# A two-layer diffusion backbone on one core: layer 1's weight sums over all of layer 0's MLP, two activation sums on VectorE, first down weights loaded early

## The chip, the core and the metric

The kernel runs on one core of a Trainium2 chip. The metric is the device time of the whole program in microseconds (us), as the median of several runs. The engines are named as in the profile: PE is TensorE's matrix multiplication and PEld its weight load, DVE is VectorE, ACT is ScalarE, POOL is GpSimd, and SP is SyncE, which in this kernel only issues transfers (DMAs). Each engine works through its own instructions in a fixed order and stops at one whose inputs or buffer are not ready; what stands behind it then waits too. "SPq" in a row of the profile is SP's queue of transfers.

## The reference, cut to what matters

A stream of 1024 latent tokens and one of 256 context tokens, 1024 channels wide, pass through two layers. Each layer has a mixer (left out here) and an MLP with a squared ReLU, 4096 hidden channels wide. Each sublayer is normalised, then scaled and shifted by a modulation that is itself a matrix product of the conditioning vectors with `w_mod`.

```python
def squared_relu_mlp(h, w1, w2):
    return jnp.square(jax.nn.relu(h @ w1)) @ w2
...
    for l in range(DEPTH):                       # DEPTH = 2
        mod_l = jnp.split((s_lat @ w_mod[l] + b_mod[l])[:, None, :], 6, axis=-1)
        mod_c = jnp.split(s_ctx @ w_mod[l] + b_mod[l], 6, axis=-1)
...
        x = x + mod_l[2] * y_l
        x = x + mod_l[5] * squared_relu_mlp(modulate(rmsnorm(x, g_norm[l, 1]), mod_l[3], mod_l[4]), w_ff1[l], w_ff2[l])
        if not last:                             # layer 0 alone: the context stream too
            xc = xc + mod_c[2] * y_c
            xc = xc + mod_c[5] * squared_relu_mlp(modulate(rmsnorm(xc, g_norm[l, 1]), mod_c[3], mod_c[4]), w_ff1[l], w_ff2[l])
    return rmsnorm(x, g_final)
```

## The kernel before, in words

**Layout and precision.** Activations lie channel by token: tiles of 128 channels and 512 tokens (token blocks `tb` 0 and 1, the latents) or 256 tokens (`tb` 2, the context). Every operand of a product is kept as two parts, a rounded one and the rest (`wsplit`: ACT makes the rounded copy at L110, DVE the difference at L111), and every product is three matmuls (`mm3`, L129 to L131).

**Layer 0's MLP** (`mlp`, L730 to L814). The 4096 hidden channels are 32 tiles, taken in 11 blocks: one of 2 tiles, then ten of 3. The first block is done token block by token block (the "lead"); the next nine are the loop `for blk in blocks[lead:-1]`; the last stands by itself. A block has two phases. In the up phase, for each hidden tile `hd`, `load` fetches its 0.5 MB of `w1` and of `w2`, each into a staging tile `st` and from there, split, into `wa` or `wb` (three buffers each), and `up` makes 128 hidden channels for the three token blocks: PE fills a bank `acc` (three of them), ACT does ReLU, square and the rounded copy (L749 to L752), DVE the difference (L753). In the down phase, for each of the 8 output tiles `fo`, `down` multiplies the block's three hidden tiles into a bank `ff` (four of them) for each token block, and DVE adds it to the residual stream (L710, `x<-ff,mod,x`). L710 has high priority, so in DVE's order it stands before side work that is written around it.

**Side work in the down phase.** Two generators are advanced by `next(...)` inside the loop over `fo`. `side` is `mods1()`: layer 1's modulation, six loads of 0.5 MB of `w_mod` per block (L97) and on DVE the products with the conditioning vectors (L181, L183). `sums` is `wsums()`: layer 1's MLP is computed with a seven-product scheme in the manner of Strassen, which needs sums of blocks of its weights. They are made here once, in 60 half-tiles: 16×2 of `w_ff1`, stored in DRAM as `su`, and 14×2 of `w_ff2`, stored as `sv`. One half-tile is two loads of 256 KB into a staging tile (L887 or L896), four additions on POOL in place (L903 to L906, 128x256 each), and a store of 512 KB (L890 or L898). SP issues all of them. In SP's queue the store waits until POOL is done, and whatever stands behind it in SP's order is issued only after it.

**One pool of staging tiles.** `st` has three buffers (`wp`, `bufs=3`), used in turn by every weight load, every `w_mod` load and every half-tile of the sums. A buffer comes free when its weight is split, when DVE has used its modulation weights, or when the half-tile's store has landed.

**Layer 1's MLP.** `right1` (L1229 to L1248) makes the seven right-hand operands out of the normalised activations `x[k, tb]`, k being a channel tile and `HK` half of the eight. `osplit` (L1207 to L1214) splits one into the rounded copy (ACT) and the difference (DVE, L1210, or L1213 where a shift is added). While this runs, PE already does the products of the first three "up units" (`lead`), operation by operation (`together`). A unit is one pair of hidden tiles through seven operations, named "1" to "7"; its left operands come through `left` (L1250 to L1280), a generator whose first step loads operations 1 and 2 and whose second loads 5/6 (as S1 and S2, into the single tile `ws`), 3 (S4) and 7/4 (S3 and A22). L1364 copies a finished product out of its bank, L1371 adds another to it, L1311 is the matmul. The up units end with unit 15, whose operations go in the order `LORDER`, and `down_unit` then does the down products by blocks `DBLK`. Layer 1's down operands come back from DRAM (`down_ops`, L1427 and L1430).

Of the kernel before, what the change touches and what calls it, by code (L numbers as in the profile page):

```python
# [9 lines left out]
F32 = mybir.dt.float32  # L10
# [7 lines left out]
P = 128  # L18
# [12 lines left out]
DBLK = ((0, 1), (2, 3, 4), (5, 6, 7), (8, 9, 10), (11, 12, 13))  # L31
NWP = 14
# [19 lines left out]
def trunk(tc, es, A, out):  # L52
    nc = tc.nc
    act, dve, pool, pe, sp = nc.scalar, nc.vector, nc.gpsimd, nc.tensor, nc.sync

    cst = es.enter_context(tc.tile_pool(name="cst", bufs=1))
    wp = es.enter_context(tc.tile_pool(name="wp", bufs=1))
# [282 lines left out]
    with ExitStack() as em, eg:  # L340
# [8 lines left out]
        for c, ks in [(c, (0, 1, 2, 3)) for c in range(3)] + [(c, (4, 5, 6, 7)) for c in range(3)] + \  # L349
                [(c, range(KT)) for c in range(3, NCH)]:  # L350
            tb, off = tok(c)
# [46 lines left out]
        for src, dst in ((LI, RI), (LF, RF)):  # L398
            for c0 in range(0, NCH, 4):
                n = min(4, NCH - c0)  # L400
# [280 lines left out]
        for g in range(3):  # L681
            v = v_proj0(g)
# [47 lines left out]
    def mlp(res, pf, pw, p2, tbs, h2, segs, finish, pre, lead, side, sums):  # L730


        l = res.l
        nh = A["ff1"].shape[1]
        first = nh % HB or HB
        blocks = [list(range(first))] + [list(range(b, b + HB)) for b in range(first, nh, HB)]

        def load(hd, w1, w2):
            if hd not in w1:
                w1[hd] = wload(A["ff1"][l, hd], (KT, P))  # L740
            if hd not in w2:
                w2[hd] = wload(A["ff2"][l, hd], (1024,), pw, "wb")

        def up(w1, tb):
            n = TBS[tb][1]
            ps = acc(n)
            proj(ps, w1, [h2[k, tb] for k in range(KT)])
            r = pf.tile([P, 512], F32, tag="s5", bufs=13, name="s5")[:, :n]
            act.activation(r, ps, AF.Relu)  # L749
            act.activation(r, r, AF.Square)  # L750
            hi, lo = actpair(tb, p2 if tb == 2 else pf, "s", (13, 3))
            act.copy(hi, r)  # L752
            dve.tensor_sub(lo, r, f(hi))  # L753
            passed(n / 100)
            return hi, lo

        def down(blk, w2, s, fo, seg, norm):
            tb, a, n = seg
            ps = aux("ff2")[:, :n]
            for j, hd in enumerate(blk):  # L760
                mm3(ps, tuple(t[:, fo * P:(fo + 1) * P] for t in w2[hd]), tuple(t[:, a:a + n] for t in s[hd, tb]),
                    j == 0, j == len(blk) - 1)
            res.update(ps, 5, fo, tb, norm, seg if norm else None)
            passed(len(blk) * n / 800)

        def ups(blk, w1, w2, s, tb):
            for hd in blk:
                load(hd, w1, w2)
                s[hd, tb] = up(w1[hd], tb)

        torder = list(dict.fromkeys(g[0] for g in segs))
        w1, w2, s = {}, {}, {}
        for i, tb in enumerate(torder):
            for bi, blk in enumerate(blocks[:lead]):
                if lead > 1:
                    w1, w2, s = {}, {}, {}
                if (0, tb) not in h2:
                    drain()
                ups(blk, w1, w2, s, tb)
                if bi == 0 and i + 1 < len(torder) and pre:  # L780
                    pre[torder[i + 1]]()
                for fo in range(KT):
                    down(blk, w2, s, fo, (tb, 0, TBS[tb][1]), False)
        for blk in blocks[lead:-1]:
            w1, w2, s = {}, {}, {}
            for hd in blk:
                load(hd, w1, w2)
                for tb in tbs:
                    s[hd, tb] = up(w1[hd], tb)
            for fo in range(KT):  # L790
                for _ in range(3):
                    next(side, None)
                for _ in range(2):
                    next(sums, None)
                for tb in tbs:
                    down(blk, w2, s, fo, (tb, 0, TBS[tb][1]), False)
        for _ in side:
            pass
        blk = blocks[-1]
        w1, w2, s = {}, {}, {}  # L800
        two = len(torder) == 2
        ups(blk, w1, w2, s, torder[0])
        for i, tb in enumerate(torder):
            if i + 1 < len(torder):
                ups(blk[:1] if two else blk, w1, w2, s, torder[i + 1])
            elif two:
                ups(blk[1:], w1, w2, s, tb)
            for seg in segs:
                if seg[0] == tb:
                    for fo in range(KT):  # L810
                        down(blk, w2, s, fo, seg, True)
                    norm_later(res.tot[seg], seg[2], acc if two and seg == segs[-1] else lone,
                               lambda r, seg=seg: finish(seg, r))
        drain()  # L814
# [12 lines left out]
    with ExitStack() as ef:  # L827
# [30 lines left out]
        for fo in range(5):  # L858
            w = ws[fo] if fo < 2 else wload(A["w_out0"][fo], (KT, P))
            for tb in (0, 1, 2):  # L860
                o, n = TBS[tb]
# [17 lines left out]
        def wsums():  # L879


            for j in range(16):
                for h in (0, 1):
                    t = wp.tile([P, 1024], F32, tag="st", bufs=3, name="st")
                    v = t.rearrange("p (i e n c) -> p i e n c", i=2, e=2, c=P)
                    for i in (0, 1):
                        sp.dma_start(v[:, i], A["ff1"][1, 2 * j + i].rearrange("p (e n) c -> p e n c", e=2)[  # L887
                            :, :, 2 * h:2 * h + 2])
                    wsum(v)
                    sp.dma_start(su[j, :, :, 2 * h:2 * h + 2], t.rearrange("p (s n c) -> p s n c", s=4, c=P))  # L890
                    yield
            for j in range(NWP):
                for h in (0, 1):
                    t = wp.tile([P, 1024], F32, tag="st", bufs=3, name="st")
                    for e in (0, 1):
                        sp.dma_start(t[:, e * 512:e * 512 + 512], A["ff2"][1, 2 * j + e, :, h * 512:h * 512 + 512])  # L896
                    wsum(t.rearrange("p (e n i c) -> p i e n c", e=2, i=2, c=P))
                    sp.dma_start(sv[j, h], t.rearrange("p (e n i c) -> p e n i c", e=2, i=2, c=P))  # L898
                    yield

        def wsum(v):
            a, b, c, d = v[:, 0, 0], v[:, 0, 1], v[:, 1, 0], v[:, 1, 1]
            pool.tensor_add(d, c, d)  # L903
            pool.tensor_sub(c, a, c)
            pool.tensor_sub(a, d, a)
            pool.tensor_sub(b, b, a)  # L906
# [322 lines left out]
    def right1(r):  # L1229

        x, d = res.x, {}
        for k in range(HK):
            scaled(k, 1, r)
            dve.tensor_sub(x[k, 0], x[k, 1], x[k, 0])
        B["5"] = [osplit(ap_, "a5", 32, x[k, 0]) for k in range(HK)]
        for k in range(HK):
            scaled(k + HK, 1, r)
            dve.tensor_sub(x[k, 0], x[k + HK, 1], x[k, 0])
        B["6"] = [osplit(po_, "o", NO, x[k, 0], shift(k + HK)) for k in range(HK)]
        B["3"] = [osplit(ap_, "a5", 32, x[k + HK, 1], shift(k + HK)) for k in range(HK)]  # L1240
        db = pf.tile([P, 16], F32, name="db")[:, 0:HK]
        dve.tensor_sub(db, mod[:, 1, 3, HK:KT, 0], mod[:, 1, 3, 0:HK, 0])
        for k in range(HK):
            pool.tensor_sub(x[k, 1], x[k + HK, 1], x[k, 1])
        B["7"] = [osplit(po_, "o", NO, x[k, 1], db[:, k:k + 1]) for k in range(HK)]
        for k in range(HK):
            pool.tensor_sub(x[k + HK, 0], x[k + HK, 0], x[k, 0])
        B["4"] = [osplit(ap_, "a2", 8, x[k + HK, 0]) for k in range(HK)]  # L1248

    def left(load, n, early=False):  # L1250
# [165 lines left out]
    def down_ops(blk, ops=WORDER):  # L1416

        nb = {}
        for op in ops:
            i = WORDER.index(op)  # L1420
            nb[op] = []
            for j in blk:
                at = (ap_, "a5", 32) if i < 4 else (po_, "o", NO)
                if i < NSPLIT:
                    w = tuple(at[0].tile([P, 512], F32R, tag=at[1], bufs=at[2], name=at[1]) for _ in range(2))
                    for e in range(2):
                        sp.dma_start(f(w[e]), f(sw[j, i, e]))  # L1427
                else:
                    v = px.tile([P, 512], F32, tag="t", bufs=5, name="t")
                    sp.dma_start(v, f(sw[j, i, 1]))  # L1430
                    w = osplit(*at, v)
                nb[op].append(w)
        return nb
# [53 lines left out]
    nxt = {}  # L1487
    for op in LORDER:
        u.run(op)
        if op == "2":  # L1490
            nxt.update(down_ops(DBLK[0], ("1", "5", "6", "3")))
        elif op == "6":
            d = down_unit(DBLK[0], 0, nxt)
            nxt.update(down_ops(DBLK[0], ("7", "2", "4")))
        elif op == "4":
            reload_x(0)
# [117 lines left out]
```

## Time and profile before

| | before |
|---|---|
| median of 3 runs | 3215.52 us (3210.82 to 3216.55) |
| the profiled execution | 3212.63 us |
| its span in the profile | 3210.9 us |
| PE busy | 2956.2 us, 92% |
| DVE busy | 1960.8 us, 61% |
| ACT busy | 1207.9 us, 38% |
| POOL busy | 310.4 us, 10% |
| bytes moved | 443.52 MB, mean 138 GB/s |
| mean granted PE clock | 0.963 |

How to read it: the span is what the profiler covers; 1.7 us of the profiled execution lie around it. A row of a view reads: time, engine, line of the code, operation, `out<-in` by the program's tile names, shape, and how often (xN); what stands in brackets is the idle time just before, and what ended it. A row of the waits reads: engine, tile and line that waited, what it waited for, then the total in us, the number of times and the longest.

### The profile page before, as it was taken

The numbers are of one execution on the slowest core, as the hardware profiler recorded it, in microseconds if no ns is written. First come the engines' busy times: TensorE is split into PE (matmuls) and PEld (weight loads), VectorE is DVE, ScalarE is ACT, GpSimd is POOL, SyncE is SP. The second block draws the span as 40 slices with busy tenths as digits, with TensorE's granted clock in tenths as the row PEclk, the third lists the DMA queues.
The fourth block names the chain that finished last, engine by engine and source line by source line (L and its number), as shares of the span: only waits on it lengthen the run. The fifth ranks groups of instructions, "written<-read, shape, count | busy, mean of one in ns | idle before, by whom it ended". The sixth has DMA issues, their size and how long they took to land.

```text
span 3210.9 us, 44648 instructions
## 1 busy us (share of the span) xinstructions
PE 2956.2 (92%) x16386; PEld 2479.8 (77%) x16386; DVE 1960.8 (61%) x3877; ACT 1207.9 (38%) x2660; POOL 310.4 (10%) x491
## 2 busy tenths in 40 slices
PE   6899999999966887999999979999999799998998
PEld 5787888788755776888888867787877578876887
DVE  5868687537343433444445568757577776656766
ACT  3335344424120221222224225556577454433332
POOL 0001011000444442000000000000000200000000
PEclk9999999999978988999999989999999899999999
DMA  6153334631565564222212143222532366687751
GB/s 207 44 161 110 109 119 148 201 103 33 164 203 184 179 203 169 79 79 66 71 58 82 56 148 95 90 74 82 178 102 96 107 223 237 240 296 225 252 183 70
DMA packets 303803, 443.52 MB, mean 138 GB/s; under 512 B 25712, under 2 KB 174816, under 8 KB 303584
## 3 DMA queue, kind: packets, MB, share of 16 engines
q1 hardware_dynamic: 300992, 436.74, 42.0%
q10 hardware_dynamic: 2592, 3.93, 0.3%
q8 instruction: 129, 2.11, 0.3%
q14 instruction: 90, 0.74, 0.1%
HBM read 330.08 MB, written 110.49 MB: 137 GB/s over the span
## 4 chain that ended last, share of the span: by engine, by line
PE 67%; DMA 12%; DVE 9%; POOL 6%; issue 3%; ACT 2%; SPq 1%; POOLq 0%; DVEq 0%; ACTq 0%
PE acc L131 9%; PE acc L129 9%; PE acc L130 9%; PE acc L1311 9%; PE bd L1311 7%; DMA st<-in_ff_dram 4%; PE ff L129 3%; PE po L1109 3%; PE ff L130 3%; PE ff L131 3%; PE S L1083 3%; DMA kd<-rh 2%; DMA qd<-rh 2%; PE pT L1104 2%; DMA su<-st 1%
## 5 line engine op out<-in xcount | busy, mean ns | idle before, releaser
L129 PE MATMUL acc<-a,wah 128*128 128x512 f32 (+1 forms) x1752 | 652.2, 372 | 36.8 <-ACT wah L110 21.9
L130 PE MATMUL acc<-a,wah 128*128 128x512 f32 (+1 forms) x1752 | 646.3, 369 | 0.0
L131 PE MATMUL acc<-a,wal 128*128 128x512 f32 (+1 forms) x1752 | 643.4, 368 | 0.0
L129 PEld LDWEIGHTS acc<-a,wah 128*128 128x128 f32 x1752 | 337.2, 192 | 87.1 <-ACT wah L110 25.9
L131 PEld LDWEIGHTS acc<-a,wal 128*128 128x128 f32 x1752 | 336.6, 192 | 47.5 <-DVE wal L111 0.5
L130 PEld LDWEIGHTS acc<-a,wah 128*128 128x128 f32 x1752 | 337.4, 193 | 45.6 <-issue 0.5
L129 PE MATMUL ff<-s,wbh 128*128 128x512 f32 (+1 forms) x768 | 280.8, 368 | 81.5 <-DVE x L710 81.5
L110 ACT CAST wah<-st 128x1024 fp32r<-128x1024 f32 (+4 forms) x129 | 120.5, 936 | 556.3 <-DMA st<-in_ff_dram 448.9
L130 PE MATMUL ff<-s,wbh 128*128 128x512 f32 (+1 forms) x768 | 277.7, 362 | 0.0
L131 PE MATMUL ff<-s,wbl 128*128 128x512 f32 (+1 forms) x768 | 276.5, 360 | 0.0
L710 DVE SCALAR_TENSOR_TENSOR x<-ff,mod,x 128x512 f32<-128x512 f32 (+1 forms) x264 | 172.0, 658 | 105.4 <-PE ff L131 103.7
L129 PEld LDWEIGHTS ff<-s,wbh 128*128 128x128 f32 x768 | 148.9, 194 | 108.6 <-DVE x L710 84.4
L111 DVE TENSOR_TENSOR wal<-st,wah 128x1024 fp32r<-128x1024 f32 (+4 forms) x129 | 138.7, 1077 | 137.7 <-ACT wah L110 137.4
L753 DVE TENSOR_TENSOR s<-s,s 128x512 fp32r<-128x512 f32 (+1 forms) x96 | 61.6, 644 | 242.5 <-ACT s L752 242.3
L1085 DVE TENSOR_REDUCE mx<-S 128x1 f32<-128x512 f32 (+1 forms) x288 | 165.4, 594 | 68.5 <-PE S L1083 67.1
L1091 ACT ACTIVATE p<-S,nm 128x512 f32<-128x512 f32 (+1 forms) x288 | 175.9, 620 | 45.1 <-DVE nm L1088 44.8
L1083 PE MATMUL S<-K,Q 128*128 128x512 f32 (+1 forms) x576 | 163.7, 384 | 14.7 <-ACT p L1091 8.2
L1311 PE MATMUL bd<-a,wbh 128*128 128x512 f32 x480 | 154.6, 403 | 18.0 <-ACT wbh L1262 8.8
L129 PE MATMUL acc<-wah,a 128*128 128x256 f32 (+1 forms) x560 | 163.1, 292 | 6.9 <-ACT a L271 4.5
L130 PEld LDWEIGHTS ff<-s,wbh 128*128 128x128 f32 x768 | 149.4, 194 | 21.1 <-issue 0.2
L131 PEld LDWEIGHTS ff<-s,wbl 128*128 128x128 f32 x768 | 148.8, 194 | 21.7
L130 PE MATMUL acc<-wal,a 128*128 128x256 f32 (+1 forms) x560 | 160.8, 289 | 0.0
(391 smaller groups left out, 5929.5 us busy)
## 6 DMA issues: line engine op xcount, KB each, us to landing
st<-in_ff_dram SPq DMA_DIRECT2D x168, 256.0 KB
st<-in_ff_dram SPq DMA_DIRECT2D x68, 512.0 KB
st<-in_w_mod_dram SPq DMA_DIRECT2D x48, 512.0 KB
a<-sw SPq DMA_DIRECT2D x84, 256.0 KB
stm<-in_w_mod_dram SPq DMA_DIRECT2D x128, 128.0 KB
su<-st SPq DMA_DIRECT2D x32, 512.0 KB
bc<-rb SPq DMA_DIRECT2D x30, 512.0 KB
sv<-st SPq DMA_DIRECT2D x28, 512.0 KB
```

The costliest lines, as they stand in the source:

```text
L110: act.copy(hi, v)
L111: dve.tensor_sub(lo, v, f(hi))
L129: pe.matmul(ps, lh, rh, start=first, stop=False)
L130: pe.matmul(ps, lh, rl, start=False, stop=False)
L131: pe.matmul(ps, ll, rh, start=False, stop=last)
L710: dve.scalar_tensor_tensor(xt, ps, mod[:, self.l, ch, fo, s:s + 1], xt, MUL, ADD)
L1083: pe.matmul(s_, Q[m][:, kind, qb * P:(qb + 1) * P], K[hh, m][:, a:a + n], start=(kind == 0), stop=(kind == 1))
L1085: dve.tensor_reduce(mx[:, i:i + 1], s_, AX, MAX)
L1091: act.activation(e[:, a:a + n], S[i], AF.Exp, bias=nm, accum_out=Z[:, m, i:i + 1])
L1104: pe.transpose(pT[:, (c - c0) * P:(c - c0 + 1) * P], p[0][:, c * P:(c + 1) * P], ident)
L1109: pe.matmul(po[:, 0:P], aT[:, (c - c0) * P:(c - c0 + 1) * P], v[c][:, hh * P:(hh + 1) * P], start=(c == 0), stop=(c == NCH - 1))
L1311: pe.matmul(ps, l_, r_, start=bool(first) and j == 0 and i == 0, stop=j == n - 1 and i == 2, skip_group_check=True)
```

## The change

Three places are changed.

1. `wsums` is written as one loop over the 16 + 14 pairs, and a half-tile now takes two steps: the first issues its loads and the four additions, the second its store. `mlp` advances `sums` once per `fo` (before: twice), and once more after each `up` of token blocks 0 and 1. A block of the loop thus takes 8 + 6 = 14 steps, seven half-tiles, instead of 16 half-tiles; 60 half-tiles need 120 steps, so they reach over all nine blocks of the loop (before: over its first 3.75). What is left is drained after the loop.
2. In `right1`, eight sums of activations go from POOL to DVE.
3. At the end of the up units, the first down unit `d` is made after operation "2" of unit 15 instead of after "6". Making a unit takes the first step of its left operands (operations 1 and 2); the added `next(d.left)` takes the second there too (5/6, 3 and 7/4), which otherwise comes when the unit runs.

```diff
@@ mlp
                 for tb in tbs:
                     s[hd, tb] = up(w1[hd], tb)
+                    if tb < 2:
+                        next(sums, None)
             for fo in range(KT):
                 for _ in range(3):
                     next(side, None)
-                for _ in range(2):
-                    next(sums, None)
+                next(sums, None)
                 for tb in tbs:
                     down(blk, w2, s, fo, (tb, 0, TBS[tb][1]), False)
-        for _ in side:
-            pass
+        for g in (side, sums):
+            for _ in g:
+                pass
@@ wsums
-            for j in range(16):
+            for j in range(16 + NWP):
                 for h in (0, 1):
...
                     wsum(v)
-                    sp.dma_start(su[j, :, :, 2 * h:2 * h + 2], t.rearrange("p (s n c) -> p s n c", s=4, c=P))
                     yield
...
+                    sp.dma_start(*keep)
                     yield
@@ right1
         for k in range(HK):
-            pool.tensor_sub(x[k, 1], x[k + HK, 1], x[k, 1])
+            dve.tensor_sub(x[k, 1], x[k + HK, 1], x[k, 1])
         B["7"] = [osplit(po_, "o", NO, x[k, 1], db[:, k:k + 1]) for k in range(HK)]
         for k in range(HK):
-            pool.tensor_sub(x[k + HK, 0], x[k + HK, 0], x[k, 0])
+            dve.tensor_sub(x[k + HK, 0], x[k + HK, 0], x[k, 0])
@@ the end of the up units
         if op == "2":
+            d = down_unit(DBLK[0], 0, nxt)
+            next(d.left)
             nxt.update(down_ops(DBLK[0], ("1", "5", "6", "3")))
         elif op == "6":
-            d = down_unit(DBLK[0], 0, nxt)
             nxt.update(down_ops(DBLK[0], ("7", "2", "4")))
```

In the changed kernel the lines behind these stand one to five further down: the sums' loads are L890 and L895 and their one store is L901, the two loads of left operands are L1294 and L1306, the sums in `right1` are L1247 and L1250, the differences of `osplit` L1213 and L1216, the addition to a kept product L1374.

**SP in layer 0's MLP.** Names are tiles with their number; `st` is a staging tile, L97 a load of modulation or MLP weights. This is the start of the down phase of the loop's first block, before:

```order
L97 DMA st_8996<-in_w_mod_dram 128x4x256
L887 DMA st_9004<-in_ff1_dram 128x2x256 x2
L887 DMA st_9012<-in_ff1_dram 128x2x256 x2
L97 DMA st_9055<-in_w_mod_dram 128x4x256
L890 DMA su_7097<-st_9004 512x1x256
L890 DMA su_7097<-st_9012 512x1x256
L887 DMA st_9061<-in_ff1_dram 128x2x256 x2
L887 DMA st_9069<-in_ff1_dram 128x2x256 x2
L887 DMA st_9126<-in_ff1_dram 128x2x256 x2
L890 DMA su_7097<-st_9061 512x1x256
```

And in the changed kernel, from the middle of a down phase into the next block's up phase:

```order
L97 DMA st_12134<-in_w_mod_dram 128x4x256
L901 DMA sv_7098<-st_12093 128x1024
L895 DMA st_12181<-in_ff2_dram 128x512 x2
L901 DMA sv_7098<-st_12181 128x1024
L97 DMA st_12223<-in_w_mod_dram 128x4x256
L97 DMA st_12262<-in_ff1_dram 128x1024
L97 DMA st_12268<-in_ff2_dram 128x1024
L895 DMA st_12306<-in_ff2_dram 128x512 x2
L901 DMA sv_7098<-st_12306 128x1024
L97 DMA st_12377<-in_ff1_dram 128x1024
L97 DMA st_12383<-in_ff2_dram 128x1024
L895 DMA st_12421<-in_ff2_dram 128x512 x2
```

Before, two or three half-tiles follow each other between two `w_mod` loads, and none stands in an up phase; now about one half-tile stands between two `w_mod` loads, and in the up phase one stands between the weights of two hidden tiles, its store ahead of the next tile's weights.

**DVE in `right1`.** `x` and `a2` are the activations, `o` and `a5` the differences of `osplit`, `bd` a bank of PE; the L1371 rows add PE's operation 6 to the kept sums of the three lead units. Before, from the last sum for operation 3 on:

```order
L1238 TENSOR_TENSOR x_21176<-a2_21734,x_21176 128x512
L1213 SCALAR_TENSOR_TENSOR o_23683<-x_21170,mod_91,o_23682 128x512
L1213 SCALAR_TENSOR_TENSOR a5_23699<-a2_21728,mod_91,a5_23698 128x512
L1213 SCALAR_TENSOR_TENSOR o_23687<-x_21172,mod_91,o_23686 128x512
L1371 TENSOR_TENSOR x_23375<-x_23375,bd_23377 128x512
L1213 SCALAR_TENSOR_TENSOR o_23691<-x_21174,mod_91,o_23690 128x512
L1371 TENSOR_TENSOR x_23589<-x_23589,bd_23591 128x512
```

In the changed kernel, from the fifth of the eight differences on:

```order
L1216 SCALAR_TENSOR_TENSOR o_23691<-x_21174,mod_91,o_23690 128x512
L1216 SCALAR_TENSOR_TENSOR a5_23707<-a2_21732,mod_91,a5_23706 128x512
L1216 SCALAR_TENSOR_TENSOR o_23695<-x_21176,mod_91,o_23694 128x512
L1216 SCALAR_TENSOR_TENSOR a5_23711<-a2_21734,mod_91,a5_23710 128x512
L1247 TENSOR_TENSOR a2_21720<-a2_21728,a2_21720 128x512
L1247 TENSOR_TENSOR a2_21722<-a2_21730,a2_21722 128x512
L1247 TENSOR_TENSOR a2_21724<-a2_21732,a2_21724 128x512
L1247 TENSOR_TENSOR a2_21726<-a2_21734,a2_21726 128x512
L1216 SCALAR_TENSOR_TENSOR o_23721<-a2_21720,db_23714,o_23720 128x512
L1250 TENSOR_TENSOR x_21178<-x_21178,x_21170 128x512
L1216 SCALAR_TENSOR_TENSOR o_23725<-a2_21722,db_23714,o_23724 128x512
L1374 TENSOR_TENSOR x_23375<-x_23375,bd_23377 128x512
```

The first addition of a finished product stood behind three differences; now eight differences, four sums and four further rows of this preparation stand ahead of it (one L1250 row, for `x_21180`, is between the last two shown). The kept product `x_23375` takes the buffer of `x_21170`, whose last reader is now the L1250 row.

**SP at the first down unit.** `ws` is the single tile for operands 5/6; `su` rows are unit 15's sums, `sv` rows the first down unit's. Before:

```order
L1291 DMA st_25942<-in_ff1_dram 128x512 x2
L1291 DMA st_26023<-su_7097 128x512
L1303 DMA ws_26179<-sv_7098 128x2x128 x2
L1412 DMA sw_23136<-x_25707 128x512
L1291 DMA st_26029<-su_7097 128x512
L1410 DMA sw_23136<-o_25789 128x512
L1291 DMA st_26029<-in_ff1_dram 128x512
```

After:

```order
L1294 DMA st_25942<-in_ff1_dram 128x512 x2
L1306 DMA st_25980<-in_ff2_dram 128x2x128 x2
L1294 DMA ws_26043<-su_7097 128x512 x2
L1415 DMA sw_23136<-x_25707 128x512
L1306 DMA st_25994<-sv_7098 128x2x128
L1413 DMA sw_23136<-o_25789 128x512
L1415 DMA sw_23136<-x_25721 128x512
```

The first down unit's operands now stand ahead of unit 15's own operands 5/6, 3 and 7/4, in the tile `ws` too.

More of the change, by code (lines that the diff above doesn't have):

```diff
@@ L879, in wsums @@
         def wsums():
-            for j in range(16):
+            for j in range(16 + NWP):
                 for h in (0, 1):
                     t = wp.tile([P, 1024], F32, tag="st", bufs=3, name="st")
[L885 to L888, printed above, removed]
+                    if j < 16:
+                        v = t.rearrange("p (i e n c) -> p i e n c", i=2, e=2, c=P)
+                        for i in (0, 1):
+                            sp.dma_start(v[:, i], A["ff1"][1, 2 * j + i].rearrange("p (e n) c -> p e n c", e=2)[
+                                :, :, 2 * h:2 * h + 2])
+                        keep = su[j, :, :, 2 * h:2 * h + 2], t.rearrange("p (s n c) -> p s n c", s=4, c=P)
+                    else:
+                        for e in (0, 1):
+                            sp.dma_start(t[:, e * 512:e * 512 + 512],
+                                         A["ff2"][1, 2 * (j - 16) + e, :, h * 512:h * 512 + 512])
+                        v = t.rearrange("p (e n i c) -> p i e n c", e=2, i=2, c=P)
+                        keep = sv[j - 16, h], t.rearrange("p (e n i c) -> p e n i c", e=2, i=2, c=P)
                     wsum(v)
-                    sp.dma_start(su[j, :, :, 2 * h:2 * h + 2], t.rearrange("p (s n c) -> p s n c", s=4, c=P))
                     yield
[L892 to L898, printed above, removed]
+                    sp.dma_start(*keep)
                     yield
```

## The prediction

> **What bounds the kernel now.** I read the page's 40 slices first, then asked for two stretches of layer 0's MLP, with and without sums, then for what waits there.
>
> ```profile
> PE   6899999999966887999999979999999799998998
> POOL 0001011000444442000000000000000200000000
> PEclk9999999999978988999999989999999899999999
> ...
> 843.60:1305.30 461.70, 358.37 (x1882) 302.39 (x1881) 182.87 (x329) 82.86 (x132) 165.12 (x212) 0.88 0.53 174
> 1305.30:1641.00 335.70, 335.70 (x1810) 287.38 (x1809) 149.83 (x262) 83.48 (x132) 0.00 (x0) 1.00 0.23 73
> ...
> 843.60:1305.30 461.70, 61.66 (x96) 0.88 0.53 174
> 1305.30:1641.00 335.70, 63.34 (x96) 1.00 0.23 73
> ```
>
> PE is busy in nine tenths of most slices, so the kernel is bound by PE, and time can only come from slices in which PE is not. The largest run of those is where POOL reads 4: the weight sums. The two stretches say how much. Columns: window, length, busy time of PE, PEld, DVE, ACT, POOL, then granted clock, DMA share, GB/s; the last two rows count DVE's L710 alone. Each stretch holds 96 updates, four blocks of 24. The four with sums took 461.70 us, the four without 335.70, in which PE was busy throughout at full clock. **The loss is 126.0 us**: 103.3 of PE idle, the rest its clock of 0.88 after idling. 83.9 us a block is PE's own time.
>
> ```profile
> PE ff L129 <- DVE x L710: 81.5, 7, 20.4
> PE acc L129 <- ACT wah L110: 18.4, 3, 9.9
> DVE av L181 <- DMA st<-in_w_mod_dram: 86.3, 5, 24.7
> DVE av L183 <- DMA st<-in_w_mod_dram: 35.8, 7, 10.1
> ...
> DVE av L183 <- DMA st<-in_w_mod_dram: 3.5, 3, 1.6
> DVE av L181 <- DMA st<-in_w_mod_dram: 1.8, 1, 1.8
> ...
> 1022.50 0.86 DVE L181 TENSOR_SCALAR av<-st,sT 128x256 f32<-128x256 f32 x1 [23.42 <-DMA st<-in_w_mod_dram]
> ...
> SPq L890 <- POOL st L906: 98.2, 32, 3.9
> SPq L898 <- POOL st L906: 83.9, 26, 5.0
> ```
>
> These are waits (total, times, longest): four rows of the stretch with sums, two of the one without, one stall of DVE, two of SP's queue. Read together they are one chain. SP's queue waits for POOL before each store (182.1 us); a `w_mod` load behind it is issued late; DVE, in order, sits at L181 for its data (122.1 us, against 5.3 in the clean stretch); the update L710 behind it does not free a bank; PE waits (81.5 us). The late weights behind the same queue give the other 18.4.
>
> ```profile
> 1004.71 3.36 DMA st<-in_ff_dram
> 1011.38 3.22 DMA su<-st
> 1027.55 0.56 SPq L890
> 1039.65 4.52 DMA st<-in_ff_dram
> ```
>
> From the chain that ended last there: a half-tile is a load of 3.36 us, four POOL additions (165.12/212 = 0.78 each, 3.12), 0.56 of issue, a store of 3.22. What SP cannot overlap is load, sum and issue: 7.04 us. Sixteen a block make 113 us, over PE's 83.9 and close to the 115.4 measured (461.70/4). So density, not their number, is what costs.
>
> **Part 1, the sums.** Work is the same: 60 half-tiles, 120 loads, 240 additions, 60 stores. Per block 7 × 7.04 = 49 us of SP's chain stand against 83.9: 35 us of margin. The staging buffers agree: a half-tile holds one for 3.36 + 3.12 + 0.56 + 3.22 = 10.3 us; 7 take 72 of the 252 buffer-us that three have per block, before 164. Half-tiles are now interleaved one by one with `w_mod` loads, so a load waits behind one sum (about 3 us), not two or three. Gain: −126.0.
>
> What is given back is that five more blocks carry sums. From below it is 0: the clean stretch has the same `w_mod` loads and no wait on PE. From above, one transfer a block ends late on PE's path: 9 × 3.36 = 30. I take half a microsecond a block, **4.5**, near the lower end because of the margin. The later store lets the next load pass it in SP's order; it can save nothing that PE feels, and costs a buffer for one step, inside the 30. What is drained after the loop is nothing: nine blocks give 126 steps for 120.
>
> DVE is the one engine that may feel the sums directly:
>
> ```profile
> L183 DVE SCALAR_TENSOR_TENSOR av<-st,sT,av 128x256 f32<-128x256 f32 x68 | 40.0, 588 | 37.9 <-DMA st<-in_w_mod_dram 37.5
> L183 DVE SCALAR_TENSOR_TENSOR av<-st,sT,av 128x256 f32<-128x256 f32 x77 | 37.2, 483 | 5.1 <-DMA st<-in_w_mod_dram 3.5
> ```
>
> The modulation product took 588 ns beside sums (800 to 1240 us) and 483 without (1280 to 1640), while L710 was no slower beside them (61.66 against 63.34 us for 96). The total of POOL's time does not change, so DVE's extra doesn't either; it is only spread. DVE has 149.83/4 = 37.5 us of work a block; if all POOL time, 7 × 3.12 = 21.8, blocked it, 59 of 83.9 would be used. Cost: 0, hidden by DVE's idle time.
>
> The Trainium skill ("SBUF — State Buffer", section "Who interferes with whom") says that a DVE instruction with both inputs in SBUF and a GpSimd instruction that reads SBUF exclude each other for a whole instruction. The rows agree in kind: L710, whose one input is in PSUM, is untouched. By the rule alone, with every lock on PE's path, the 21.8 us a block would make the sum some 3290; the rival below takes half of it.
>
> **Part 2, eight sums on DVE.**
>
> ```profile
> 2548.05 1.28 DVE L1234 TENSOR_TENSOR x<-a,x 128x512 f32<-128x512 f32 x2
> 2556.54 1.76 DVE L1238 TENSOR_TENSOR x<-a,x 128x512 f32<-128x512 f32 x1
> 2559.55 3.33 DVE L1238 TENSOR_TENSOR x<-a,x 128x512 f32<-128x512 f32 x2
> 2562.80 1.75 DVE L1213 SCALAR_TENSOR_TENSOR o<-x,mod,o 128x512 fp32r<-128x512 f32 x1
> ...
> 2566.14 1.75 DVE L1213 SCALAR_TENSOR_TENSOR o<-x,mod,o 128x512 fp32r<-128x512 f32 x1
> 2567.81 0.68 DVE L1371 TENSOR_TENSOR x<-x,bd 128x512 f32<-128x512 f32 x1
> 2568.41 0.74 DVE L1213 SCALAR_TENSOR_TENSOR o<-x,mod,o 128x512 fp32r<-128x512 f32 x1
> ...
> 2553.26 2.81 POOL L1244 TENSOR_TENSOR a<-a,a 128x512 f32<-128x512 f32 x1 [8.66 <-DVE a L1218]
> 2563.96 3.38 POOL L1247 TENSOR_TENSOR x<-x 128x512 f32<-128x512 f32 x2
> ...
> 2564.63 0.58 ACT L1364 COPY x<-acc 128x512 f32<-128x512 f32 x1 [4.96 <-DVE o L1213]
> 2565.27 1.22 PE L1311 MATMUL acc<-o,wbh 128*128 128x512 f32 x2 [7.38 <-ACT x L1364]
> 2568.54 1.22 PE L1311 MATMUL bd<-a,wbh 128*128 128x512 f32 x2 [2.05 <-DVE x L1371]
> ```
>
> While POOL adds (2553.26 to 2567.3), DVE's rows with two SBUF inputs take 1.75 us, alone 0.64 to 0.74 (of three L1213 rows at 1.75 the first and the last are shown). Without POOL it saves 1.12 + 2.05 + 3 × 1.01 = 6.2 us and gains 8 × 0.64 = 5.1: a net −1.1. But order matters more. PE waits twice here, for the copy L1364 and for the addition L1371. The last L1238 would end at about 2562.80 − 1.12 − 2.05 − 0.4 (an earlier row) = 2559.2. Now eight differences at 0.66 (the spacing of 2568.41 after L1371's 0.60), four sums at 0.60, then two pairs (0.66 + 0.60) stand ahead of the first addition: 2559.2 + 5.3 + 2.4 + 2.5 = 2569.4, against 2567.81. The copy, released one pair earlier (2568.2), ends in time. **+1.6**; bounds −1.1 (only the net) and +5.1 (all eight sums on the path).
>
> **Part 3, the first down unit's weights.**
>
> ```profile
> 2838.00:2872.00 34.00, 34.00 (x149) 27.46 (x149) 17.80 (x27) 12.92 (x23) 0.00 (x0) 1.00 0.96 310
> 2836.28 0.95 SPq L1303 DMA_DIRECT2D ws<-sv  x2
> 2895.10 0.95 SPq L1303 DMA_DIRECT2D ws<-sv  x2
> 2901.54 1.22 PE L1311 MATMUL bd<-a,wbh 128*128 128x512 f32 x2 [8.77 <-ACT wbh L1262]
> ```
>
> PE is busy 34.00 of 34.00 us where the first down unit's operands are loaded and its products start, so there is no wait to remove. The wait of 8.77 us comes at the block's last unit, whose load (2895.10) is not moved. That excludes a gain at this place. What can be lost: unit 15's own 5/6, 3 and 7/4 now load behind up to seven transfers more, where DMA is already 0.96 busy. What hides that is the unit's operations 1 and 2, whose operands are not moved; if this cover is too short, one load of 3.36 us ends late. I take **0**, because the queue runs ahead of a PE without gaps; bounds 0 and +3.4.
>
> **The sum.** 3212.63 − 126.0 + 4.5 + 1.6 + 0 = 3092.7 for an execution like the profiled one; the median of the runs lay 2.9 above it, so **3095.6**. Its own range, by the bounds of the four terms, is 3088 to 3128.
>
> **Rivals.**
>
> *Half-way.* Modulation loads still come late in down phases. DVE's waits were 122.1/4 = 30.5 us a block at sixteen half-tiles; four now fall into a down phase, 7.6, of which I let the free banks cover a third: 5 us × 9 = 45 instead of 4.5, time 3136. For: each load still stands behind a store that waits for POOL. Against: the margin.
>
> *The loss goes by number.* If each half-tile costs 126.0/60 = 2.1 us wherever it stands, nothing is gained: 3217. For: the same transfers and additions. Against: PE idles only behind loads that the queue had delayed by several sums.
>
> *Slower: the up phase becomes a chain.* An up unit is half a block's work over three:
>
> ```profile
> L131 PE MATMUL ff<-s,wbl 128*128 128x512 f32 (+1 forms) x289 | 102.4, 354 | 0.0
> L131 PE MATMUL acc<-a,wal 128*128 128x512 f32 (+1 forms) x288 | 101.9, 354 | 0.0
> ```
>
> So 83.9/2/3 = 14.0 us of PE. Between two tiles' weights SP now waits for a load and a sum. Were everything serial, the chain would be three loads, the sum and the issue: 3 × 3.36 + 3.12 + 0.56 = 13.8, just hidden; at 4.52 a load 17.2, and 27 units lose 86 (3182). The gain is gone at 14.0 + 120/27 = 18.4 us a unit; at 19.0 the time is 3230, slower than before. For: loads of 4.52 exist. Against: weights are issued two at once and ahead of PE, and late weights cost only 18.4 us in the dense stretch.
>
> *DVE locked.* Half of 21.8 us a block on PE's path: 98 us, 3194. Against: L710 is not slowed.
>
> **How the numbers follow.** Forecast 0.79; half-way 0.12; by number 0.03; chain 0.03 (a third of it slower than before); locked 0.03. A change under 0.2% (6 us) could not be told from none. Faster: 0.79 + 0.12 + 0.02 + 0.03 = 0.96; same 0.03; slower 0.01, which I raise to 0.02 at the expense of faster. The range runs from 3084 (the lower bounds, less the 4.7 by which the lowest of the runs lay under their median) to 3136, so that it takes in the half-way case; outside lie about 0.15.
>
> **What would show it.** Right: POOL reads 2 over about nine slices (755 us) instead of 4 over five; PE reads 9 in all of the MLP at a clock of 1.00, ten blocks at 84 us; DVE's waits for `w_mod` fall from 122 us to under 20; SP's waits for POOL stay near 3 us a store and harm nobody; DVE's rows in `right1` read 0.64 to 0.74, and PE's second wait there ends 1.6 us later against the first sums. Wrong: PE waits for L710 in down phases (half-way) or for `wah` in up phases (chain), or a total of such waits near 100 us over nine blocks (by number).

## The result, and the profile after

| | before | after |
|---|---|---|
| median | 3215.62 us (3210.82 to 3216.55, 4 runs) | 3103.78 us (3095.96 to 3108.78, 4 runs) |
| ratio of the runs, 95% interval | | 0.9653 [0.963, 0.9675] |
| the profiled execution | 3212.63 us | 3095.96 us |
| its span | 3210.9 us | 3094.2 us |
| mean granted PE clock | 0.963 | 0.981 |

The change made the kernel faster by 3.5%. The time of 3103.8 lies within the range on record (3084 to 3136), 8.2 us above the forecast of 3095.6. The same three rows of the 40 slices:

```profile
PE   6899999999999999999999799999999799989998
POOL 0002011001122222222100000000000000000000
PEclk9999999999999999999999899999999899999999
```

POOL reads 2 over eight slices and 1 around them where it read 4 over five, its late 2 (`right1`) is gone, and PE reads 9 through all of the MLP. The stretches that answer to the two of before are blocks 1 to 4 and 5 to 8 of the MLP (counted from 0), from first update to first update (columns as before: window, length, PE, PEld, DVE, ACT, POOL, clock, DMA share, GB/s):

```profile
843.90:1186.20 342.30, 339.07 (x1881) 289.61 (x1880) 174.69 (x328) 82.11 (x132) 87.13 (x108) 1.00 0.47 151
1186.20:1522.90 336.70, 336.22 (x1809) 287.15 (x1808) 158.92 (x262) 81.69 (x132) 89.72 (x108) 1.00 0.46 157
```

The engines' waits in the same time (total, times, longest):

```profile
PE acc L129 <- ACT s L749: 3.5, 2, 3.2
PE ff L129 <- DVE x L710: 0.2, 1, 0.2
DVE av L183 <- DMA st<-in_w_mod_dram: 16.6, 5, 4.7
DVE av L181 <- DMA st<-in_w_mod_dram: 1.9, 2, 1.3
```

And of the waits of SP's queue, the longest:

```profile
SPq L901 <- POOL st L909: 181.2, 54, 4.5
```

The first four blocks fell from 461.70 to 342.30 us, the next four rose from 335.70 to 336.70 though they now carry 27 of the 60 half-tiles (108 additions, four each). Over the eight blocks PE's waits for L710 went from 81.5 to 0.2 us, and DVE's for `w_mod` from 127.4 (122.1 and 5.3) to 18.5. SP still waits 3.4 us for POOL at each store (181.2/54), against 3.1 before (182.1/58); PE now feels it at one place of note.

This place is a stall in the loop's second block (89.25 us between first updates, 83.7 to 84.7 between the others of the loop). SP's queue there:

```profile
967.34 0.56 SPq L901 DMA_DIRECT2D su<-st  x1
972.29 0.81 SPq L97 DMA_DIRECT2D st<-in_ff_dram  x2
```

The same two transfers in the chain that ended last, with their flight, and what follows them there:

```profile
967.34 4.94 DMA su<-st
972.29 3.65 DMA st<-in_ff_dram
979.33 1.14 DVE wbl L111
980.48 3.98 DMA st<-in_ff_dram
```

ACT and PE some us later, in the order of time:

```profile
984.49 1.04 ACT L110 CAST wah<-st 128x1024 fp32r<-128x1024 f32 x1 [5.58 <-DMA st<-in_ff_dram]
986.08 0.79 PE L129 MATMUL acc<-a,wah 128*128 128x512 f32 x1 [3.23 <-ACT s L749]
```

And two windows, of the stall and of what follows it:

```profile
983.00:986.10 3.10, 0.02 (x1) 0.02 (x1) 0.53 (x1) 1.58 (x3) 2.34 (x4) 1.00 0.66 248
986.10:990.00 3.90, 3.90 (x10) 3.14 (x11) 2.52 (x3) 3.84 (x7) 0.00 (x0) 0.57 0.78 257
```

The staging buffer of a hidden tile's weights is held by a half-tile until its store has landed (967.34 + 4.94 = 972.28). The next weights come late too, because their buffer is one of these and comes free only when DVE has split it (`wbl`, up to 980.47). They land at 984.46; until then ACT sits at their copy (L110), the ReLU behind it does not free a bank `acc`, and PE waits 3.23 us. It then runs 3.9 us at a clock of 0.57. The Trainium skill ("TensorE: Matmul & The Clock Gate", Part 1) has PE drop to half rate after an idle window of about 3.4 us. Here the drop came after 3.23 us, and in a run below (stored at once) the same wait of 3.20 us brought none: the clock read 1.00 over the 3.6 us behind it.

### The profile page after: what moved, and what is told of

It is laid out like the page before. It is cut to its first block, busy times and chain, and to the rows that moved or that the text cites. A ratio compares the mean times of both kernels' runs of the same rounds, so it can differ in the third digit from the quotient of the medians.

```text
span 3094.2 us, 44658 instructions
## 1 busy us (share of the span) xinstructions
PE 2933.4 (95%) x16386; PEld 2461.5 (80%) x16386; DVE 1959.3 (63%) x3885; ACT 1205.1 (39%) x2660; POOL 306.0 (10%) x483
## 4 chain that ended last, share of the span: by engine, by line
PE 73%; DVE 11%; DMA 9%; POOL 2%; ACT 2%; issue 2%; SPq 1%; POOLq 0%; DVEq 0%; ACTq 0%
PE acc L131 11%; PE acc L129 11%; PE acc L130 11%; PE acc L1314 8%; PE bd L1314 6%; PE ff L129 4%; PE ff L130 4%; PE ff L131 4%; PE po L1112 3%; PE S L1086 3%; DMA st<-in_ff_dram 2%; DMA kd<-rh 2%; PE pT L1107 2%; DMA qd<-rh 1%; DMA t<-sw 1%
## 5 line engine op out<-in xcount | busy, mean ns | idle before, releaser
L110 ACT CAST wah<-st 128x1024 fp32r<-128x1024 f32 (+4 forms) x129 | 120.4, 935 | 483.2 <-DMA st<-in_ff_dram 375.1
L129 PE MATMUL ff<-s,wbh 128*128 128x512 f32 (+1 forms) x768 | 274.3, 359 | 0.2 <-DVE x L710 0.2
L130 PE MATMUL ff<-s,wbh 128*128 128x512 f32 (+1 forms) x768 | 272.4, 355 | 0.0
L710 DVE SCALAR_TENSOR_TENSOR x<-ff,mod,x 128x512 f32<-128x512 f32 (+1 forms) x264 | 171.0, 658 | 96.1 <-PE ff L131 94.8
L129 PE MATMUL acc<-wah,a 128*128 128x256 f32 (+1 forms) x560 | 161.8, 290 | 6.5 <-ACT a L271 4.1
L129 PEld LDWEIGHTS ff<-s,wbh 128*128 128x128 f32 x768 | 144.8, 189 | 24.5 <-DVE x L710 1.0
L130 PEld LDWEIGHTS ff<-s,wbh 128*128 128x128 f32 x768 | 145.2, 189 | 20.7 <-DVE s L753 0.6
L131 PE MATMUL acc<-wah,a 128*128 128x256 f32 (+1 forms) x560 | 159.6, 290 | 0.3 <-DVE a L272 0.2
```

What stands on the lines that cost most here:

```text
L110: act.copy(hi, v)
L129: pe.matmul(ps, lh, rh, start=first, stop=False)
L130: pe.matmul(ps, lh, rl, start=False, stop=False)
L131: pe.matmul(ps, ll, rh, start=False, stop=last)
L710: dve.scalar_tensor_tensor(xt, ps, mod[:, self.l, ch, fo, s:s + 1], xt, MUL, ADD)
```

## The experiments

| run | median us | ratio to before, 95% interval | MLP: first to last L710, us |
|---|---|---|---|
| before | 3215.5 | | 1006.3 |
| changed kernel | 3103.8 | 0.9653 [0.963, 0.9675] | 887.9 |
| part 1 alone | 3101.3 | 0.9648 [0.9628, 0.9667] | 887.2 |
| sixteen a block, stored late | 3216.1 | 1.0006 [0.9993, 1.0018] | 1005.8 |
| eight a block, all in the down phase | 3142.9 | 0.9777 [0.9757, 0.9797] | 930.2 |
| stored at once | 3102.7 | 0.9649 [0.9629, 0.967] | 888.0 |
| eight a block, six in the up phase | 3112.0 | 0.9673 [0.9659, 0.9688] | 888.6 |
| no additions | 3093.0 | 0.9618 [0.9603, 0.9632] | 881.5 |
| part 2 alone | 3217.7 | 1.0008 [0.9998, 1.0017] | 1009.2 |
| part 3 alone | 3216.4 | 1.0002 [0.9992, 1.0012] | 1007.3 |
| as eight in the down phase, modulation in the up phase | 3171.6 | 0.9871 [0.9852, 0.9891] | 957.7 |
| changed, fourth sums early | 3094.8 | 0.9635 [0.961, 0.966] | 889.9 |
| the same, sums placed anew (1) | 3097.3 | 0.964 [0.9615, 0.9664] | 890.9 |
| the same, sums placed anew (2) | 3092.4 | 0.961 [0.9597, 0.9623] | 882.5 |

The last column is read from each trace. Where the MLP's rate and places are the same it repeats within 3 us (887.2, 887.9, 888.0 and 889.9; in the kernel before 1006.3, 1007.3 and 1009.2), so it tells more than the total: the first three of these executions differ by 9.5 us in span (3100.4, 3094.2, 3103.7). Matched matmul by matmul, that of part 1 alone stands 0.2 us ahead of the changed kernel's at the MLP's end and 4.3 behind it after layer 1's attention; the other one comes 3.2 late to the MLP's end and is 10.7 late there. In these three the scatter arises mostly in layer 1's mixer and at the kernel's start.

**Part 1 alone.** Parts 2 and 3 are as in the kernel before.

> Part 1 alone; parts 2 and 3 undone. Density theory (SP's chain of load, sum and issue must fit into PE's time for a block): the same gain of about 118 us in the MLP, 3093 to 3107 us, PE idle under 10 us in the MLP; in right1 the waits of before (7.38 and 2.05 us) come back. Rival, the loss goes by number of half-tiles: 3215 us, and parts 2 and 3 made the gain.

3101.3 us, MLP 887.2: the whole gain is part 1's. The loss does not go by number.

**Sixteen a block, stored late.**

```diff
-                next(sums, None)            # and the one after each up
+                for _ in range(4):
+                    next(sums, None)
```

> The changed kernel with four steps per output tile and none in the up phase: sixteen half-tiles a block as before, all in the down phase, but the store one step later. Density theory: 16 x 7.04 = 113 us a block again, over 83.9, so the loss comes back: 3190 to 3220 us. Rival, the store issued at once was the cause (it blocked SP's queue): the gain stays, 3095 to 3110 us.

3216.1 us, blocks of 125, 115, 114 and 107 us: the loss is back in full, with the store a step later. **Stored at once** is the reverse, the rate of the change with the old place of the store:

```diff
                     wsum(v)
-                    yield
                     sp.dma_start(*keep)
                     yield
+                    yield
```

> The changed kernel at the same rate and places, but with the store in the same step as the sums (the second step is empty). Density theory: no change against the changed kernel, 3095 to 3110 us. Rival, the later store carries the gain: most of it is lost, over 3150 us.

3102.7 us, MLP 888.0. The later store does nothing; rate and place do it. The run with sixteen differs in both, since none of its half-tiles stands in an up phase; the next run has nearly the rate of the change (eight half-tiles a block for seven), all in the down phase.

**Eight a block, all in the down phase** (two steps per `fo`, none after an up).

> The changed kernel with two steps per output tile and none in the up phase: eight half-tiles a block, all in the down phase. Density theory by block: 8 x 7.04 = 56 us fit into 83.9, no loss, 3095 to 3110 us. Rival, density counts by phase (the down phase alone has 41.9 us of PE): 14 us lost in each of 7.5 blocks, about 3200 us, so the steps in the up phase were needed.

3142.9 us: neither. 42.3 us of MLP are lost, though 8 × 7.04 = 56 us is far below 83.9. So the block is not the unit in which room must be counted. ACT, DVE and PE at the longest stall but one:

```profile
1070.48 1.04 ACT L110 CAST wah<-st 128x1024 fp32r<-128x1024 f32 x1 [46.30 <-DMA st<-in_ff_dram]
1071.55 1.42 DVE L111 TENSOR_TENSOR wal<-st,wah 128x1024 fp32r<-128x1024 f32 x1 [9.07 <-ACT wah L110]
1072.90 2.18 DVE L710 SCALAR_TENSOR_TENSOR x<-ff,mod,x 128x256 f32<-128x256 f32 x4
1073.42 0.80 PE L129 MATMUL ff<-s,wbh 128*128 128x512 f32 x1 [8.32 <-DVE x L710]
```

PE's wait is one for an update, as before the change, but DVE did not wait for modulation weights: it stood at the difference of the next block's first weights (`wal`), which the sums had made late, with four updates behind it.

**Eight a block, six in the up phase** (two steps after each up of token blocks 0 and 1, one at every second `fo`).

> Eight half-tiles a block as in the run with eight in the down phase, but six of them in the up phase (two a hidden tile) and two in the down phase. Theory of density by phase: an up unit is 14.0 us of PE, SP's chain there would be 2 x 7.04 + 2 x 3.36 = 20.8 us, so up to 20 us a block are short; eight in the down phase were short 14 us a block and lost 5.6 of them (42 us in 7.5 blocks), so at the same share 8 a block here: about 3160 us, PE waiting in up phases. Rival, only modulation loads behind sums cost time and they stand in the down phase: about 3100 us. Second rival, nothing can be prefetched across the chain: all 20 us a block, 3250 us, slower than before.

The theory of this run, that the up phase is as short of room, fell: from the third block of the loop on there is no idle PE at all, with two half-tiles per hidden tile, and the first two lose 7 us (the second alone lost 5 in the changed kernel). The time of 3112.0 has another part. Two half-tiles now stand in POOL's order ahead of a small operation of the norm that the MLP starts with (POOL's rows):

```profile
751.99 0.72 POOL L908 TENSOR_TENSOR st<-st 128x256 f32<-128x256 f32 x1 [7.34 <-DMA st<-in_ff_dram]
754.28 0.71 POOL L227 TENSOR_TENSOR q<-r,nhalf 128x2 f32<-128x2 f32 x1
```

and PE's:

```profile
756.67 1.22 PE L232 MATMUL lone<-dg,ones 128*128 128x256 f32 x2 [8.38 <-DVE dg L230]
```

PE waits 8.38 us for a norm that waits for sums that wait for their load. In the changed kernel there is no such wait.

**No additions.** The changed kernel without the four POOL additions, so the stored sums are not sums.

> The changed kernel with the four additions on GpSimd left out: loads and stores are unchanged, the stored sums are not sums. Theory: the additions are 3.12 of the 7.04 us of SP's chain, so the one stall that is left (3.2 us idle, about 5 us longer third block) goes, and the blocks take 84 us: MLP about 5 to 8 us shorter, 3090 to 3102 us. Rival, the stall is the slow store (4.94 us) holding its staging buffer: it stays, within 2 us of the changed kernel. DVE locked by GpSimd: more than 8 us gained.

MLP 881.5, 6.4 us shorter, and the second block takes 83.9 us: the stall left goes when the sums' chain loses POOL's time, though its stores are still made. A lock of DVE by POOL that PE feels is thereby at most about these 6.4 us, of which 5.4 are the second block's (89.25 against 83.89).

**The modulation in the up phase.** Eight half-tiles in the down phase again:

```diff
                     s[hd, tb] = up(w1[hd], tb)
+                    for _ in range(3):
+                        next(side, None)
             for fo in range(KT):
-                for _ in range(3):
-                    next(side, None)
```

> The run with eight half-tiles in the down phase (3142.9 us), but with the modulation's steps (its w_mod loads and DVE products) moved into the up phase, three after each up. Theory: what costs time is a w_mod load that stands behind sums in a down phase, where DVE's updates stand behind its data; with none there the 42 us go: 3095 to 3112 us, PE's waits for L710 near 0. Rival, eight chains of 7.04 us are too many for a down phase of 42 us whatever else loads: about 3143 us, with PE waiting for weights (wah) in its place. A new wait is possible: DVE's L753 in the up phase behind w_mod data.

My theory here failed: without a `w_mod` load among the sums the loss is larger, 957.7 us. The rival holds only in that the loss stays: it had 3143 us, not 3171.6, and PE waiting for `wah`, where PE waits for L710 still. SP's queue in one down phase, its first and last rows of sums and the weights among and behind them:

```profile
1106.86 1.21 SPq L889 DMA_DIRECT2D st<-in_ff_dram  x2
...
1147.28 0.63 SPq L97 DMA_DIRECT2D st<-in_ff_dram  x1
1151.84 0.57 SPq L900 DMA_DIRECT2D su<-st  x1
1152.45 0.63 SPq L97 DMA_DIRECT2D st<-in_ff_dram  x1
```

ACT, DVE and PE there:

```profile
1152.06 1.04 ACT L110 CAST wah<-st 128x1024 fp32r<-128x1024 f32 x1 [22.25 <-DMA st<-in_ff_dram]
1153.13 1.23 DVE L111 TENSOR_TENSOR wal<-st,wah 128x1024 fp32r<-128x1024 f32 x1 [13.29 <-ACT wah L110]
1155.07 0.79 PE L129 MATMUL ff<-s,wbh 128*128 128x512 f32 x1 [8.51 <-DVE x L710]
```

From the first load to the last store eight half-tiles take 45.0 us, 5.6 each, a little over the 41.9 that PE has in a down phase (half of 83.9). The weights that ACT waits for (issued at 1147.28, behind the stores of seven of the eight) come late, DVE sits at `wal` for 13.29 us, and L710 behind it keeps PE waiting 8.51. The comparison is rough: this chain began 24 us before the first update of its down phase (1131.06). It leaves 3.1 us a block short, and 69.8/7.5 = 9.3 were lost. What the modulation's move added to that was not taken apart. Nor was it shown whether SP's order or the three staging buffers set the 5.6 us, since no run had a fourth buffer; in the run with eight, over the MLP, SP waited 188.1 us for POOL before stores and 104.6 us for stores to land before it could load again.

**Parts 2 and 3 alone**, each in the kernel before.

> Part 2 alone in the kernel before. Own theory: DVE's rows there fall from 1.75 to 0.74 us, PE's 7.38 us wait grows to about 12, the one of 2.05 goes; from the first of the three waits to the next gap after them (53.3 us before) it is 0.5 to 2 us longer; total 3214 to 3219 us, not to be told from before. Rival, GpSimd's lock on DVE was on the path: 4 us or more gained.

> Part 3 alone in the kernel before. Own theory: PE has no wait where the first down unit starts, so nothing changes: 3211 to 3220 us, the 8.77 us wait of the block's last unit stays. Rival, the later loads of unit 15's own operands end late: one or two new waits of 1 to 3.4 us on L1311 ahead of the first down unit.

Neither total can be told from before. PE's wait in `right1` with part 2 alone:

```profile
2576.88 1.22 PE L1311 MATMUL acc<-o,wbh 128*128 128x512 f32 x2 [11.57 <-ACT x L1364]
```

In the changed kernel, PE:

```profile
2449.29 1.22 PE L1314 MATMUL acc<-o,wbh 128*128 128x512 f32 x2 [11.88 <-ACT x L1367]
2450.48 1.22 PE L1314 MATMUL bd<-a,wbh 128*128 128x512 f32 x2
```

and DVE:

```profile
2438.30 1.28 DVE L1241 TENSOR_TENSOR x<-a,x 128x512 f32<-128x512 f32 x2
2444.81 2.49 DVE L1247 TENSOR_TENSOR a<-a,a 128x512 f32<-128x512 f32 x4
2449.74 0.68 DVE L1374 TENSOR_TENSOR x<-x,bd 128x512 f32<-128x512 f32 x1
```

And with part 1 alone, where the eight sums are on POOL, PE:

```profile
2452.13 1.22 PE L1314 MATMUL acc<-o,wbh 128*128 128x512 f32 x2 [7.78 <-ACT x L1367]
2455.40 1.22 PE L1314 MATMUL bd<-a,wbh 128*128 128x512 f32 x2 [2.05 <-DVE x L1374]
```

DVE's sums on `a` and `x` take 0.62 to 0.68 us, the operations beside them are as fast, the wait of 2.05 us goes, and the other grows by about 4. From the first of the three waits to the next gap behind them the stretch is 54.1 to 55.1 us in the eight runs with part 2 in this order (mean 54.6), and 53.3, 54.1 and 54.3 in the three without: 0.7 us longer, less than its scatter. For part 3 a stretch of 1300 matmuls around the first down unit is 319.2, 318.6 and 319.3 us with it, 317.6, 319.5 and 317.1 without: no difference beyond the scatter of 2 us. The late wait stays, 8.43 us with part 3 alone and in the changed kernel:

```profile
2783.49 1.22 PE L1314 MATMUL bd<-a,wbh 128*128 128x512 f32 x2 [8.47 <-ACT wbh L1265]
```

**Fourth sums early.** The changed kernel with one loop of `right1` drawn into another:

```diff
             dve.tensor_sub(x[k, 0], x[k + HK, 1], x[k, 0])
+            dve.tensor_sub(x[k + HK, 0], x[k + HK, 0], x[k, 0])
...
-        for k in range(HK):
-            dve.tensor_sub(x[k + HK, 0], x[k + HK, 0], x[k, 0])
```

> The changed kernel with the four sums for operation 4 written directly behind those for operation 6, so that the buffer that the kept product waits for is read out earlier. Theory: PE's 11.88 us wait in right1 is DVE's order; the copy then waits only for the second difference, the wait falls to 4 to 6 us and the stretch to the next gap (54.7 us) to 48 to 51. Rival, DVE's total work there bounds it: the time comes back as a later wait, within 1.5 us of 54.7. In the total 4 to 7 us: 3097 to 3100 against 3103.8, at the edge of what can be told.

```profile
2447.88 1.22 PE L1313 MATMUL acc<-o,wbh 128*128 128x512 f32 x2 [4.83 <-ACT x L1366]
```

The wait falls from 11.88 to 4.83 us, and the time for the same 450 matmuls, from ten before the three waits on, from 128.2 to 122.0. A later wait of 0.81 us is new; to the gap that was the next before, the stretch is 48.2 us. Over the eight runs with part 2 in its first order these matmuls take 127.4 to 129.9 us (mean 128.3), over the three with this reordering 122.0 to 123.7 (mean 122.9): 5.4 us stay gained. The totals' intervals overlap those of the changed kernel.

**Sums placed anew.** On top of that, (1) three half-tiles in each of the first three blocks, then eight and a half; (2) three in the first two, then eight, six of them in the up phase. The diff is that of (2); (1) has `bi < 3`, and `bi > 2 and fo < 5` in the last condition:

```diff
-                    if tb < 2:
-                        next(sums, None)
+                    if tb < 2:
+                        for _ in range(1 if bi < 2 else 2):
+                            next(sums, None)
...
-                next(sums, None)
+                if bi > 1 and fo % 2:
+                    next(sums, None)
```

> The same reordering, and the sums placed by what the runs so far showed: in the first three blocks of the loop three half-tiles, all in the up phase; in the six others eight and a half, six in the up phase and five steps in the down phase. Theory: the stall of the loop's second block (5 us) goes and none comes: updates of the MLP from 887.9 to 881 to 883 us, total 3088 to 3097. Rival, eight and a half a block bring waits back in the later blocks: MLP 888 us or more.

> The reordering of the run with the early fourth sums, and the sums placed so that each phase has room: in the first two blocks of the loop three half-tiles, all in the up phase; in the other seven eight, six in the up phase and two in the down phase, which was the place without any loss from the third block on. Theory: no wait of PE in the MLP; its updates span 881 to 883 us (887.9 changed kernel, 889.9 with the reordering alone), total 3086 to 3093, in the middle 7 us under the reordering alone (3094.8). Rival, the third block stalls as the second did, wherever the sums begin in the down phase: MLP 886 us or more.

(1) removes the second block's stall and brings others in blocks 6, 8 and 9, counted from 0 (MLP 890.9): its rival holds. A count by phase does not foretell this: two and a half half-tiles at 5.6 us are 14 us of the down phase's 41.9, and the up phase is as in (2). Five steps also leave every second block with a half-tile loaded but not stored, in one of three buffers, at its end; that this is the reason was not tested. (2) has two half-tiles a down phase, not two and a half, and PE has one wait left in these nine blocks (two windows, which cover them):

```profile
845.40:1266.90 421.50, 420.80 (x2329) 360.05 (x2328) 217.69 (x391) 102.06 (x165) 112.45 (x136) 1.00 0.48 154
1266.90:1586.70 319.80, 319.80 (x1746) 274.05 (x1745) 153.66 (x256) 76.98 (x123) 76.49 (x92) 1.00 0.45 150
```

The waits of PE there:

```profile
PE acc L129 <- ACT s L749: 0.7, 1, 0.7
```

MLP 882.5 us, 0.961 [0.9597, 0.9623] of before: this version beats the changed kernel, whose interval lies wholly above, by about 11 us; the two traces show 5.4 of them in the MLP and 5.4 in the 450 matmuls around `right1`'s waits (128.2 and 122.8).

## Why the prediction was right, point by point

**Part 1, −126.0 + 4.5.** Right in its mechanism and nearly in its size. The MLP fell from 1006.3 to 887.9 us: −118.4, so 7.6 was given back, not 4.5; the 3.1 between them are no more than the scatter of that span. Some 5 of the 7.6 is the one stall in the second block, priced at a flat half microsecond a block. It is the rival's chain in the up phase, at one place: weights behind a sum's buffer, ACT before PE. That rate and place cost, and not the number, is shown by part 1 alone and by the runs with sixteen and with eight in the down phase; that the later store adds nothing, by the run that stores at once.

**The margin of 35 us a block** is the step of the argument that failed, without harm to the sum. Eight a block would by it have kept 28 us of margin, and lost 42 us when all stood in the down phase. The phase matters: 5.6 us a half-tile back to back are 45 us of SP's time for eight, against 41.9 us of PE, with the next weights in the same queue and the same buffers. The change puts four in the down phase (22 us) and three in the up phase. That this count is the reason is argued: it has the sign of the loss, but neither its size nor the waits of the run with eight and a half.

**The up phase as a chain** was priced too high at 13.8 to 17.2 us a unit: with twice the sums there (six a block) PE does not wait from the third block on.

**DVE beside POOL, 0.** Within the 6.4 us that the run without additions gained; L710 took 62.4 and 61.6 us for 96, as before.

**Part 2, +1.6.** From the first of the three waits' matmuls (2549.45 before, 2429.72 after) to the first in a bank `bd` behind the others: 19.09 us before, 20.76 after, +1.7. By the later gap it is 0.7, eight runs against three; both within the bounds. The first addition (L1374) starts 20.02 us behind the first of these matmuls, where L1371 started 18.36 behind it: the +1.6 was DVE's order, as worked out. PE no longer stops for that addition; its one wait there is now for the copy, and is longer. That the wait for the kept product's buffer sets it was shown by the reordering.

**Part 3, 0.** Not to be told from 0; the wait of 8.77 stayed at 8.47.

**The sum** was 3092.7 for an execution like the profiled one; that took 3095.96, the 3.1 of part 1 too much. The other 5 us to the median are the choice of base: the profiled execution of before stood 2.9 below its median, that of after 7.8, as the lowest of its four. That the sum comes so near is in part luck: three executions with the same MLP differ by up to 9.5 us.

## What to carry to other kernels

When side work shares one in-order queue and one pool of staging buffers with loads that the critical engine needs, its cost goes by its rate and place, not by its amount: spread it over all phases until no wait is left. Counting the room phase by phase gives a first guess; a run must tell, since half a half-tile more a block brought waits back here. Look for the victim one step away: PE waited for an update, the update stood behind an instruction waiting for quite another load. When work moves to a faster engine, ask what its new place in that engine's order holds back; two loops drawn together were worth more than the move.

## What the runs showed that I had not expected

Two half-tiles per hidden tile fit into the up phase (14.0 us of PE) without a wait, while eight in a down phase of 41.9 us cost 5.6 us a block. Beside POOL's adds one DVE operation took 1.75 us instead of 0.74, yet moving the adds to DVE gained nothing: PE's first wait there grew from 7.4 to 11.9 us.
